# Norm and LayerNorm roots and the gated embedding kept in PSUM, with half of the residual adds of the embedding stages on GpSimd

## The chip, the cores and the metric

The kernel runs on the eight cores of one Trainium2 chip. The work is data parallel: each core has one row of 2048 prompt tokens and sixteen sequences of eight sample tokens. The metric is the device time of the slowest core in microseconds (us). Most executions agree within 0.3%. Some fall into a slower state, in which the cores of one die have a lower granted TensorE clock (the share of the full clock that the profile records), whatever the kernel is. Only fast runs are compared here, and lengths of stages are read from cores whose mean clock was 0.996 to 0.998 unless another is given. A core with such a mean can still have a lower clock within one stage; where that matters, the clock in the stage is given.

TensorE is called PE in the profile, VectorE DVE, ScalarE ACT and GpSimd POOL.

## The reference, cut to what matters

A step is two layers. Each has an FFN, a mixer, a second FFN and then a gated input embedding. The change acts mostly on that last part, which is called the embedding stage here.

```python
def rmsnorm(x, g):
    ...
    inv = lax.rsqrt(jnp.mean(xf * xf, axis=-1, keepdims=True) + NORM_EPS)
    return (xf * inv * g.astype(jnp.float32)).astype(x.dtype)
...
for i in range(DEPTH):                       # DEPTH = 2, D_MODEL = 1024
    ...                                      # FFN, mixer, FFN, each with its norm
    gate = jax.nn.sigmoid(rmsnorm(x, norm_ple[i]) @ w_ple_gate[i])
    emb = rmsnorm(p[i].astype(x.dtype) @ w_ple_proj[i], norm_ple_proj[i])
    x = x + gate * emb
y = rmsnorm(x, norm_final)
```

## The kernel before

The residual stream X stays in SBUF, transposed: eight chunks of 128 channels for each block of tokens. There are four blocks of 512 columns (x_43 to x_46 in the profile) and one sample block of 128 (x_47). The normalised input H (h_48 to h_52) feeds the matmuls. All accumulators come from a pool of eight PSUM banks, named ps.

An embedding stage does this for each chunk `mo` of each block `b`:

```python
pz, pe_ = bank(), bank()                         # two PSUM banks
mm(pz[:, 0:n], ...)                              # gate: 8 matmuls
mm(pe_[:, 0:n], ...)                             # embedding: 2 matmuls
th = scr()                                       # SBUF scratch
act(th[:, 0:n], pz[:, 0:n], AF.Tanh, scale=0.5)  # ScalarE
bfree(pz)
dve_stt(th[:, 0:n], th[:, 0:n], 1.0, pe_[:, 0:n], ALU.add, ALU.mult)      # VectorE: product
bfree(pe_)
dve_stt(X[b][:, mo, :], th[:, 0:n], GPPH[:, l * 8 + mo:l * 8 + mo + 1], X[b][:, mo, :],
        ALU.mult, ALU.add)                                                # VectorE: residual
sfree(th)
nm[b].chunk(mo, 2.8)                             # the next norm's square of this chunk
```

The last call places a square of the new X chunk into ScalarE's program, and later a matmul with a matrix of ones that sums the squares. The first argument after `mo` is a lag. It is no wait at run time. The program is written out ahead of time, with a running count of PE time, and the lag says after how much of that time the square goes into ScalarE's instruction order. A chunk is 2.38 us of PE, so a square with lag 2.8 stands a little more than a chunk behind. In the timelines below one later tanh stands between a chunk's own tanh and its square.

When all eight squares of a block are summed, the root is taken and eight products give H:

```python
self.wait = {"pe": 4.0, "dve": 1.2, "pool": 1.0}[mode]   # from the square to its sum, same clock
...
def chunk(self, mo, lag=0.8):
    ...
    defer(lag * k, square, self.tag)                     # k = 1 for 512 columns

def rsqrt(self):
    rs = scr()                                           # the root goes to SBUF
    act(rs[:, 0:n], self.pb[:, 0:n], AF.Abs_reciprocal_sqrt, bias=NORM_EPS)
    bfree(self.pb)
    st = 0.7 if n == 512 else 0.3
    ...                                                  # for c in 8: at 2.0 + st * c
    dve_stt(out[b][:, c, :], X[b][:, c, :], pcol(self.gname, c), rs[:, 0:n], ALU.mult, ALU.mult)
```

## Time and profile before

Before took 2615.22 us (median of the three fast of four runs, 2614.91 to 2615.65; the fourth was slow, 3135.62, and the median of all four is 2615.43).

From the page (the summary of the profiled execution), which is of a core of the die at clock 0.992, the engines' busy time and share of the span and, last, the chain of waits by engine:

```profile
span 2623.8 us, 34959 instructions; the slowest of 8 cores (2608.9 to 2623.8 us)
PE 2576.8 (98%) x14375; PEld 1247.0 (48%) x14375; DVE 1155.4 (44%) x2039; ACT 708.4 (27%) x1257; POOL 168.2 (6%) x254
...
PE 93%; DVE 4%; ACT 2%; DMA 1%; issue 1%; SPq 0%; ACTq 0%; POOL 0%; DVEq 0%; POOLq 0%
```

PE is nearly always busy, so only places where it waits can give time. One such place is the pair of embedding stages. Each stage is taken from the end of the second FFN's last residual add on the sample block to the end of the last gated residual add of that block. The windows view of core 1 (clock 0.997) for the two stages has each engine's busy time:

```profile
core 1: us, PE busy (x) PEld busy (x) DVE busy (x) ACT busy (x) POOL busy (x), PEclk, DMA share, GB/s
1206.90:1305.90 99.00, 95.49 (x506) 44.97 (x503) 80.55 (x139) 61.60 (x104) 5.33 (x11) 1.00 0.19 32
2510.60:2599.30 88.70, 82.78 (x441) 40.00 (x439) 74.15 (x128) 56.54 (x98) 0.46 (x1) 0.98 0.27 87
```

VectorE is busy 81% of layer 0's stage and ScalarE 62%. The waits of PE in layer 0's stage (engine, tile, what it waited for: total, times, longest) are few:

```profile
PE ps L553 <- DVE scr_96 L523: 1.5, 1, 1.5
PE ps L553 <- DVE scr_95 L523: 0.8, 1, 0.8
PE ps L553 <- DVE scr_94 L523: 0.5, 1, 0.5
```

One more of 0.5 us (`scr_93`) falls at its end.

By the timeline of PE, the eight gate matmuls of that chunk had ended at 1264.28 us, so it was held back for 6.2 us:

```profile
1262.39 1.89 PE L553 MATMUL ps<-h_51,ring 128*128 128x512 bf16 x8
...
1269.09 1.90 PE L553 MATMUL ps<-h_51,ring 128*128 128x512 bf16 x8 [1.49 <-DVE scr_96 L523]
```

The second line is the stage's longest wait of PE. It ended with a VectorE product, as the prediction has it.

### The profile page before, as it was taken

What the parts mean: (1) busy time and instruction counts of PE and PEld (TensorE: products, weight loads), DVE (VectorE), ACT (ScalarE), POOL (GpSimd) and SP (SyncE); (2) the same over time, 40 slices, a digit from 0 to 9 for tenths busy, and PEclk for the clock granted to TensorE, in tenths of its full rate; (3) what the DMA queues carried; (4) which work ended last, traced back from release to release, by engine and by line L of the source; (5) the groups of instructions that cost most, each with busy time, mean ns of one, the idle gap of its engine ahead of it and who ended that gap; (6) DMA issues with size and microseconds to landing.
All of it is one profiled execution on the core that took longest, in us unless ns stands there. A gap on an engine that the chain in (4) does not pass through costs nothing.

```text
span 2623.8 us, 34959 instructions; the slowest of 8 cores (2608.9 to 2623.8 us)
## 1 busy us (share of the span) xinstructions
PE 2576.8 (98%) x14375; PEld 1247.0 (48%) x14375; DVE 1155.4 (44%) x2039; ACT 708.4 (27%) x1257; POOL 168.2 (6%) x254
## 2 busy tenths in 40 slices
PE   7999999999999999999999999999999999999996
PEld 2444544444454454444444454445444444544443
DVE  5432334755632222268722222267667312222687
ACT  5210112336621001125521001123333210011254
POOL 0000000012400000000000000000005000000000
PEclk9999999999999999999999999999999999999998
DMA  8320421055442132112042031103310320322113
GB/s 195 55 44 1 65 37 32 16 103 122 86 69 39 18 56 38 33 29 46 7 71 41 17 60 29 33 13 49 56 33 6 57 53 17 57 37 41 21 22 137
DMA packets 53311, 127.18 MB, mean 48 GB/s; under 512 B 9504, under 2 KB 24608, under 8 KB 53024
## 3 DMA queue, kind: packets, MB, share of 16 engines
q0 software_dynamic: 23584, 92.55, 21.1%
q1 hardware_dynamic: 28848, 31.29, 4.4%
q8 instruction: 113, 1.85, 0.3%
q10 hardware_dynamic: 720, 1.11, 0.1%
q14 instruction: 46, 0.38, 0.0%
HBM read 196.61 MB, written 10.62 MB: 79 GB/s over the span
## 4 chain that ended last, share of the span: by engine, by line
PE 93%; DVE 4%; ACT 2%; DMA 1%; issue 1%; SPq 0%; ACTq 0%; POOL 0%; DVEq 0%; POOLq 0%
PE ps L553 93%; DMA x_43<-xT 0%; DVE h_48 L523 0%; DVE h_49 L523 0%; ACT L508 0%; DVE h_50 L523 0%; DVE x_46 L523 0%; DMA ring<-wts 0%; DVE x_45 L523 0%; DMA x_44<-xT 0%; DVE v L523 0%; DVE x_44 L523 0%; DVE scr_95 L516 0%; DVE h_51 L523 0%; ACT h_51 L510 0%
## 5 line engine op out<-in xcount | busy, mean ns | idle before, releaser
L553 PE MATMUL ps<-h_48,ring 128*128 128x512 bf16 x1892 | 432.5, 382 | 12.8 <-DMA ring<-wts 12.8
L553 PE MATMUL ps<-h_49,ring 128*128 128x512 bf16 x1892 | 433.2, 382 | 2.3 <-DVE h_49 L528 1.8
L553 PE MATMUL ps<-h_50,ring 128*128 128x512 bf16 x1892 | 428.8, 381 | 2.3 <-DVE h_50 L523 1.6
L553 PE MATMUL ps<-h_51,ring 128*128 128x512 bf16 x1892 | 427.7, 380 | 3.2 <-DVE scr_96 L523 1.5
L553 PEld LDWEIGHTS ps<-h_49,ring 128*128 128x128 bf16 x1892 | 185.6, 98 | 229.3 <-issue 14.6
L553 PEld LDWEIGHTS ps<-h_50,ring 128*128 128x128 bf16 x1892 | 185.4, 98 | 227.4 <-issue 8.0
L553 PEld LDWEIGHTS ps<-h_51,ring 128*128 128x128 bf16 x1892 | 184.8, 98 | 228.2 <-issue 4.7
L553 PEld LDWEIGHTS ps<-h_48,ring 128*128 128x128 bf16 x1892 | 182.2, 98 | 220.5 <-issue 23.4
L577 POOL DMA_DIRECT2D ring<-wts x152 | 80.8, 538 | 2057.4 <-PE ps L553 1967.9
L553 PE MATMUL ps<-hid_54,ring 128*128 128x512 bf16 x736 | 164.3, 380 | 0.0
L553 PE MATMUL ps<-hid_56,ring 128*128 128x512 bf16 x736 | 163.7, 379 | 0.0
L553 PE MATMUL ps<-hid_55,ring 128*128 128x512 bf16 x736 | 163.7, 379 | 0.0
L553 PE MATMUL ps<-hid_53,ring 128*128 128x512 bf16 x736 | 162.8, 379 | 0.0
L510 ACT ACTIVATE scr_97<-ps 128x512 f32<-128x512 f32 (+1 forms) x135 | 77.1, 571 | 309.5 <-PE ps L553 300.4
L510 ACT ACTIVATE scr_95<-ps 128x512 f32<-128x512 f32 (+1 forms) x130 | 67.7, 521 | 293.9 <-PE ps L553 293.9
L510 ACT ACTIVATE scr_96<-ps 128x512 f32<-128x512 f32 (+1 forms) x119 | 68.7, 577 | 241.4 <-PE ps L553 239.2
L553 PE MATMUL ps<-h_52,ring 128*128 128x128 bf16 x1892 | 124.3, 220 | 5.0 <-DVE scr_96 L523 3.1
L553 PEld LDWEIGHTS ps<-h_52,ring 128*128 128x128 bf16 x1892 | 115.0, 98 | 28.0 <-DVE scr_96 L523 3.3
L553 PEld LDWEIGHTS ps<-hid_54,ring 128*128 128x128 bf16 x736 | 72.2, 98 | 86.8 <-issue 1.2
L553 PEld LDWEIGHTS ps<-hid_56,ring 128*128 128x128 bf16 x736 | 72.0, 98 | 86.8
L553 PEld LDWEIGHTS ps<-hid_55,ring 128*128 128x128 bf16 x736 | 71.9, 98 | 86.7
L553 PEld LDWEIGHTS ps<-hid_53,ring 128*128 128x128 bf16 x736 | 71.6, 98 | 84.1
(502 smaller groups left out, 2150.3 us busy)
## 6 DMA issues: line engine op xcount, KB each, us to landing
ring<-wts POOLq DMA_DIRECT2D x110, 512.0 KB, 9.7
ring<-wts POOLq DMA_DIRECT2D x40, 768.0 KB, 8.0
rr<-u SPq DMA_DIRECT2D x48, 135.0 KB, 3.1
rr<-u SPq DMA_DIRECT2D x16, 134.8 KB, 3.5
x_44<-xT SPq DMA_DIRECT2D x8, 256.0 KB, 6.0
x_45<-xT SPq DMA_DIRECT2D x8, 256.0 KB, 11.4
x_46<-xT SPq DMA_DIRECT2D x8, 256.0 KB, 12.5
yT<-x_43 SPq DMA_DIRECT2D x8, 256.0 KB, 2.1
```

Of the source, the lines that this page charges most:

```text
L510: return e.activation(out=out, in_=in_, func=func, **kw)
L553: ins = e.matmul(o_, l, r, start=st, stop=sp)
L577: S.op(eng, lambda e: e.dma_start(out=out, in_=in_), reads=[in_], writes=[out], dma_sem=sem, dma_total=total, extra_deps=extra)
```

## The change

The intent is to take work off VectorE, which had the most to do next to PE, and to keep GpSimd's new work from disturbing it.

- Roots of the norms, of the embedding's own norm and of the LayerNorm stay in the PSUM bank that held the sum, so a norm product reads one SBUF input and one PSUM input.
- For every second 512-column chunk ScalarE scales the tanh by the gain (`gp * th + gp`), VectorE multiplies by the embedding, and GpSimd adds to the residual.
- For the other chunks the product is written back to its PSUM bank, and that bank is freed after the residual.
- The lag of the square is 4.2 for GpSimd's chunks, and the time from square to sum is 4.5.

```diff
-            self.wait = {"pe": 4.0, "dve": 1.2, "pool": 1.0}[mode]
+            self.wait = {"pe": 4.5, "dve": 1.2, "pool": 1.0}[mode]
...
-            rs = scr()
-            act(rs[:, 0:n], self.pb[:, 0:n], AF.Abs_reciprocal_sqrt, bias=NORM_EPS)
-            bfree(self.pb)
+            rs = self.pb
+            act(rs[:, 0:n], rs[:, 0:n], AF.Abs_reciprocal_sqrt, bias=NORM_EPS)
...
-                        sfree(rs)
+                        bfree(rs)
...                          (the same for the embedding's norm and the LayerNorm)
-            dve_stt(th[:, 0:n], th[:, 0:n], 1.0, pe_[:, 0:n], ALU.add, ALU.mult)
-            bfree(pe_)
-            dve_stt(X[b][:, mo, :], th[:, 0:n], GPPH[:, l * 8 + mo:l * 8 + mo + 1], X[b][:, mo, :],
-                    ALU.mult, ALU.add)
-            sfree(th)
-            nm[b].chunk(mo, 2.8)
+            gp = GPPH[:, l * 8 + mo:l * 8 + mo + 1]
+            pooled = mo % 2 == 0 and b < SB
+            if pooled:
+                act(th[:, 0:n], th[:, 0:n], AF.Identity, bias=gp, scale=gp)
+                dve_tt(th[:, 0:n], th[:, 0:n], pe_[:, 0:n], ALU.mult)
+                bfree(pe_)
+                pool_tt(X[b][:, mo, :], th[:, 0:n], X[b][:, mo, :], ALU.add)
+                sfree(th)
+            else:
+                dve_stt(pe_[:, 0:n], th[:, 0:n], 1.0, pe_[:, 0:n], ALU.add, ALU.mult)
+                sfree(th)
+                dve_stt(X[b][:, mo, :], pe_[:, 0:n], gp, X[b][:, mo, :], ALU.mult, ALU.add)
+                bfree(pe_)
+            nm[b].chunk(mo, 4.2 if pooled else 2.8)
```

More of the change, by code (lines that the diff above doesn't have):

```diff
@@ L801, in s1 @@
                 SQ.put(r)
-            rs = scr()
+            rs = pb
             act(rs[:, 0:n], pb[:, 0:n], AF.Abs_reciprocal_sqrt, bias=NORM_EPS)
-            bfree(pb)
             def s2():
@@ L808, in s2 @@
                     dve_tt(HID[b][:, k, :], pt[:, k, 0:n], rs[:, 0:n], ALU.mult)
-                sfree(rs)
+                bfree(rs)
                 if b + 2 < NB:
@@ L964, in stats @@
                     LNP.put(vv)
-                mu, msq, rs = scr(), scr(), scr()
+                mu, msq, rs = scr(), scr(), p2
                 act(mu[:, 0:n], p1[:, 0:n], AF.Copy)
@@ L972, in stats @@
                     if j == 0:
-                        dve_tt(msq[:, 0:n], p2[:, 0:n], msq[:, 0:n], ALU.subtract)
-                        bfree(p2)
-                        act(rs[:, 0:n], msq[:, 0:n], AF.Abs_reciprocal_sqrt, bias=LN_EPS)
+                        dve_tt(p2[:, 0:n], p2[:, 0:n], msq[:, 0:n], ALU.subtract)
                         sfree(msq)
+                        act(rs[:, 0:n], p2[:, 0:n], AF.Abs_reciprocal_sqrt, bias=LN_EPS)
                 sfree(mu)
@@ L983, in ln1 @@
                             scale=pcol("ln_gain", j))
-                    sfree(rs)
+                    bfree(rs)
                 defer(3.0, ln1, tag)
```

## The prediction

> **What bounds the kernel.** TensorE: the page gives PE 98% of a 2623.8 us span, and the chain of waits is 93% matmuls. The holes in the PE timeline of core 5:
> - even mixer (640 to 700 us): 3.8 us idle;
> - embedding stage of layer 0 (1208 to 1312): about 4.4 us of waits, 1.5 of it in block 3 for a VectorE product that frees a bank, most of the rest around the sample block;
> - embedding stage of layer 1 (2518 to 2610): 0.6, 1.5, then 0.6 and 3.1 us waiting for VectorE in the last, 128-column block, which spans 13.2 us for about 6 us of matmuls;
> - head (about 18 us) and tail (2610 to 2624), hardly touched.
>
> In the embedding stages a 512-column chunk costs PE 2.38 us (11 matmuls at 0.216). VectorE spends about 1.39 us on the chunk's two scalar_tensor_tensor (0.68, 0.75) plus 0.66 for one normalisation product of an earlier block, in bursts of four (2.7 us). Each norm's two table loads and root cost ScalarE about 3.2 us and starve VectorE, which recovers too slowly: PE waits in block 3, and VectorE is 3 to 5 us late at the sample block.
>
> **The change.** For half the chunks VectorE loses the 0.75 us residual and keeps one product (0.68). GpSimd gains an add of about 1.16 us (its lone adds in the even mixer). ScalarE gains a pass of about 0.80 us: the trace has 0.80 for an activation with two pointer operands, 0.72 with one, 0.60 to 0.63 with none, agreeing with the Trainium skill, "ScalarE: Activation LUTs", "What ACT_TABLE_LOAD costs" (about 93 ns per pointer). Per 512 block VectorE falls from about 16.4 to 13.5 us, ScalarE rises from about 12.5 to 15, PE stays 19.
>
> rs in PSUM does not itself speed a product (0.69 from PSUM, 0.68 from SBUF). It should remove contention: norm products that overlap GpSimd's adds average 0.87 to 0.93 (h_49, h_50) against 0.745, which fits the skill's "SBUF — State Buffer", "SBUF: two separate sides" (GpSimd locks out a VectorE op with two SBUF inputs). So the new GpSimd adds should be nearly free to VectorE.
>
> The price: each norm keeps a PSUM bank some 7 us longer. When an embedding stage starts, accumulators and roots leave about 4 banks for chunks of 2 each, while VectorE there is up to 6 us behind: 1 to 3 us of new PE waits in all, there and in the even mixer.
>
> **Sum (estimates from these numbers).** Layer 0 embedding -3 us. Layer 1: -2 at block 3, -5 at the sample block. Even mixer -1 to +1. New bank waits +2. About -8 us, 0.3%: 2607 us, range 2599 to 2616. Faster by over 2%: 1%; within 2%: 98%; slower: 1%.
>
> **What would show it.** The PE waits of block 3 vanish; the last 128-column block takes 7 to 9 us; VectorE's busy time in an embedding stage falls by about 12 us, GpSimd's rises by about 19; norm products in the even mixer return to 0.745. Signs of a wrong step: PE waiting for a norm product to free a bank; squares late behind GpSimd; residual adds well over 1.2 us.
>
> **What would make it wrong.** More bank waits than thought (then no gain or a small loss); ScalarE, in order, blocked by squares that wait for GpSimd; the later squares and sums (+0.5 us) pushing a norm onto the critical path, above all at the end, where 13 us follow the last matmul.

## More of the kernel before

A piece of core 1's (start, duration, what; in brackets the idle time before it and what ended that):

```profile
1269.92 0.63 ACT L510 ACTIVATE sq_88<-x_45 128x512 bf16<-128x512 f32 x1 [2.98 <-DVE x_45 L523]
1270.45 0.58 ACT L510 ACTIVATE scr_94<-ps 128x512 f32<-128x512 f32 x1
1271.30 0.63 ACT L510 ACTIVATE sq_92<-x_45 128x512 bf16<-128x512 f32 x1 [0.27 <-DVE x_45 L523]
1271.84 0.58 ACT L510 ACTIVATE scr_97<-ps 128x512 f32<-128x512 f32 x1
```

ScalarE stood idle for 2.98 us, because the next instruction in its order was a square (`sq_88<-x_45`) whose residual was not written yet. The tanh of a later chunk (`scr_94<-ps`) followed at once after it.

## The result, and the profile after

After took 2620.6 us (median of four fast runs, 2620.39 to 2622.42), against 2615.22. The ratio is 1.0022, with a 95% interval of 1.0002 to 1.0042. Here and below a ratio is the mean time of one kernel's fast runs over that of the other's fast runs of the same rounds, so it is not quite the ratio of the medians quoted. The total lies within 2%, as the prediction said was likely, but on the wrong side: 5 us slower where 8 us faster was expected, and above the range.

The page after, the slowest core, now at clock 0.997:

```profile
span 2619.2 us, 34719 instructions; the slowest of 8 cores (2613.9 to 2619.2 us)
PE 2551.5 (97%) x14124; PEld 1243.5 (47%) x14375; DVE 1122.7 (43%) x2007; ACT 731.5 (28%) x1289; POOL 205.2 (8%) x286
...
PE 88%; DVE 5%; ACT 3%; DMA 2%; issue 1%; POOL 0%; ACTq 0%; DVEq 0%; SPq 0%; POOLq 0%
```

This trace lacks 251 matmul records (14124 of 14375), so PE's smaller busy time means nothing. The work moved as planned: VectorE has 32.7 us less, ScalarE 23.1 us more, GpSimd 37.0 us more. In the chain PE's share fell by 5 points, a part of which may come from the missing records; VectorE, ScalarE and DMA gained one point each, as rounded.

The windows view of core 1 for the two embedding stages after:

```profile
1203.10:1305.80 102.70, 95.56 (x504) 44.74 (x503) 70.03 (x123) 73.18 (x120) 25.20 (x26) 1.00 0.19 31
2510.00:2601.20 91.20, 82.78 (x440) 39.91 (x438) 63.71 (x113) 68.07 (x114) 20.83 (x17) 0.98 0.27 84
```

VectorE lost 10.5 us in layer 0's stage and 10.4 us in layer 1's, and yet the stages grew from 99.0 to 102.7 us and from 88.7 to 91.2 us. The other stages give at most a little back: the even mixer took 204.1 to 205.5 us on the four cores of die 0 before and 203.5 to 205.0 us after, and the tail went from 14.2 to 14.0 us (core 1). The FFNs and the odd mixer are equal within the spread of their cores.

The waits of PE in layer 0's stage after, where the sum is 7.1 us against 3.3 us before:

```profile
PE ps L553 <- DVE x_47 L523: 2.1, 4, 0.6
PE ps L553 <- DVE h_49 L523: 1.5, 1, 1.5
PE ps L553 <- DVE h_51 L523: 1.2, 1, 1.2
PE ps L553 <- ACT scr_93 L510: 0.8, 1, 0.8
PE ps L553 <- DVE scr_95 L516: 0.8, 1, 0.8
PE ps L553 <- ACT scr_97 L510: 0.4, 1, 0.4
PE ps L553 <- DVE h_50 L523: 0.3, 1, 0.3
```

Three kinds are new. PE waits for norm products (`h`), which free the root's bank, for residuals (`x_47`), which free the product's bank, and for tanh (`ACT scr`), which free the gate's bank.

The timelines of core 1 show how a tanh comes late. PE, ScalarE, VectorE and GpSimd, one fence each:

```profile
1261.84 1.89 PE L553 MATMUL ps<-h_51,ring 128*128 128x512 bf16 x8
...
1265.84 1.90 PE L553 MATMUL ps<-h_51,ring 128*128 128x512 bf16 x8 [1.47 <-DVE h_49 L523]
```

```profile
1263.73 0.58 ACT L510 ACTIVATE scr_96<-ps 128x512 f32<-128x512 f32 x1
1267.83 0.63 ACT L510 ACTIVATE sq_88<-x_45 128x512 bf16<-128x512 f32 x1 [3.52 <-POOL x_45 L519]
1268.37 0.58 ACT L510 ACTIVATE scr_93<-ps 128x512 f32<-128x512 f32 x1
```

```profile
1263.07 2.71 DVE L523 SCALAR_TENSOR_TENSOR h_49<-x_44,par,ps 128x512 bf16<-128x512 f32 x4
1265.70 0.68 DVE L516 TENSOR_TENSOR scr_97<-scr_97,ps 128x512 f32<-128x512 f32 x1
...
1269.83 0.69 DVE L516 TENSOR_TENSOR scr_93<-scr_93,ps 128x512 f32<-128x512 f32 x1 [2.05 <-ACT scr_93 L510]
```

```profile
1266.53 1.27 POOL L519 TENSOR_TENSOR x_45<-scr_97,x_45 128x512 f32<-128x512 f32 x1 [5.33 <-DVE scr_97 L516]
```

Read them as one chain. The gate matmuls of the first PE line ended at 1263.73 us, and their tanh is `scr_93`. The product of `scr_97` stood behind a burst of four norm products on VectorE. GpSimd could then start its add, and ended at 1267.80. Only then could ScalarE do the square of that chunk, for which it had stood idle 3.52 us. The tanh of `scr_93` came after the square, 4.6 us after its matmuls, and VectorE, whose next instruction was the product of `scr_93`, stood idle 2.05 us for the scaled `scr_93`. PE in the meantime had run out of banks: its next gate waited 1.47 us for the same burst of norm products, whose root held the bank. VectorE's idle time in the stage rose from 99.0 - 80.6 = 18.4 us to 102.7 - 70.0 = 32.7 us, so it was not short of time.

### The profile page after: what moved, and what is told of

Its sections match the earlier page's. It is cut to its first block, busy times and chain, and to the rows that moved or that the text cites. A ratio compares the mean times of both kernels' runs of the same rounds, so it can differ in the third digit from the quotient of the medians.

```text
span 2619.2 us, 34719 instructions; the slowest of 8 cores (2613.9 to 2619.2 us)
## 1 busy us (share of the span) xinstructions
PE 2551.5 (97%) x14124; PEld 1243.5 (47%) x14375; DVE 1122.7 (43%) x2007; ACT 731.5 (28%) x1289; POOL 205.2 (8%) x286
## 4 chain that ended last, share of the span: by engine, by line
PE 88%; DVE 5%; ACT 3%; DMA 2%; issue 1%; POOL 0%; ACTq 0%; DVEq 0%; SPq 0%; POOLq 0%
PE ps L553 88%; ACT L508 1%; DMA ring<-wts 1%; DVE h_50 L523 1%; DVE h_51 L523 1%; DVE x_46 L523 0%; DMA x_43<-xT 0%; DVE ps L523 0%; DMA xscr_67<-st_sc 0%; DVE v L523 0%; ACT scr_93 L510 0%; DVE h_49 L523 0%; ACT ps L510 0%; DVE h_48 L523 0%; DVE x_45 L523 0%
## 5 line engine op out<-in xcount | busy, mean ns | idle before, releaser
L553 PE MATMUL ps<-h_48,ring 128*128 128x512 bf16 x1835 | 419.1, 380 | 19.9 <-DMA ring<-wts 14.9
L553 PE MATMUL ps<-h_49,ring 128*128 128x512 bf16 x1844 | 424.3, 379 | 6.5 <-DVE h_51 L523 2.6
L553 PE MATMUL ps<-h_50,ring 128*128 128x512 bf16 x1873 | 424.8, 379 | 5.7 <-ACT scr_93 L510 1.6
L553 PE MATMUL ps<-h_51,ring 128*128 128x512 bf16 x1841 | 423.2, 379 | 6.8 <-DVE x_44 L523 1.5
L553 PEld LDWEIGHTS ps<-h_51,ring 128*128 128x128 bf16 x1892 | 184.5, 98 | 227.9 <-DVE x_44 L523 2.0
L553 PEld LDWEIGHTS ps<-h_50,ring 128*128 128x128 bf16 x1892 | 184.6, 98 | 227.4 <-ACT scr_93 L510 2.5
L553 PEld LDWEIGHTS ps<-h_49,ring 128*128 128x128 bf16 x1892 | 184.4, 98 | 226.8 <-DVE h_51 L523 3.5
L553 PEld LDWEIGHTS ps<-h_48,ring 128*128 128x128 bf16 x1892 | 181.3, 98 | 223.4 <-issue 16.4
L553 PE MATMUL ps<-hid_56,ring 128*128 128x512 bf16 x720 | 162.9, 379 | 0.9
L553 PE MATMUL ps<-hid_54,ring 128*128 128x512 bf16 x720 | 162.9, 379 | 0.8
L553 PE MATMUL ps<-hid_55,ring 128*128 128x512 bf16 x723 | 162.7, 379 | 0.6
L553 PE MATMUL ps<-hid_53,ring 128*128 128x512 bf16 x720 | 161.4, 379 | 0.8
L510 ACT ACTIVATE scr_93<-ps 128x512 f32<-128x512 f32 (+1 forms) x118 | 61.9, 524 | 355.9 <-PE ps L553 352.1
L510 ACT ACTIVATE scr_96<-ps 128x512 f32<-128x512 f32 (+1 forms) x118 | 67.0, 568 | 228.4 <-PE ps L553 226.6
L553 PEld LDWEIGHTS ps<-h_52,ring 128*128 128x128 bf16 x1892 | 114.8, 98 | 27.1 <-DVE x_45 L523 2.5
L510 ACT ACTIVATE scr_95<-ps 128x512 f32<-128x512 f32 (+1 forms) x101 | 51.7, 511 | 239.3 <-PE ps L553 229.1
L510 ACT ACTIVATE scr_94<-ps 128x512 f32<-128x512 f32 (+1 forms) x102 | 58.0, 568 | 206.3 <-PE ps L553 196.9
L553 PEld LDWEIGHTS ps<-hid_55,ring 128*128 128x128 bf16 x736 | 72.0, 98 | 86.8
L553 PEld LDWEIGHTS ps<-hid_56,ring 128*128 128x128 bf16 x736 | 72.0, 98 | 86.9
L553 PEld LDWEIGHTS ps<-hid_54,ring 128*128 128x128 bf16 x736 | 72.1, 98 | 86.5
```

What stands on the lines that cost most here:

```text
L510: return e.activation(out=out, in_=in_, func=func, **kw)
L553: ins = e.matmul(o_, l, r, start=st, stop=sp)
```

## The experiments

Two explanations stood against each other from the start.

- **Queue**: ScalarE runs its instructions in order, and a square that waits for a late residual holds back later tanh, and with them their banks. The change makes the residual later, so it should hold more of them. The Trainium skill, "PSUM — Partial Sum Buffer", section "Engine vs sequencer instructions", says that the queues of ScalarE, VectorE and GpSimd are strict FIFO. The timelines above agree, with their 2.98 and 3.52 us.
- **Banks**: roots and products that stay in PSUM take banks from PE's rotation.

A third one, that ScalarE simply has too much work (its pass), was kept as a rival too. The table has what the runs showed in layer 0's stage, on one undisturbed core each, and is the map for what follows. "Blocked" is ScalarE's idle time that ended with a residual (the sum of those lines of its waits in the stage), "starved" its idle time that ended with PE, and "PE waits" sums PE's waits. "Held" is the mean time from the end of a chunk's eight gate matmuls to the start of its tanh, over the 32 chunks of 512 columns, worked out from the timelines of PE and ScalarE.

| kernel | layer 0 stage | layer 1 stage | ScalarE busy | blocked | starved | PE waits | held |
|---|---|---|---|---|---|---|---|
| before (lag 2.8) | 99.0 | 88.7 | 61.6 | 33.6 | 2.2 | 3.3 | 2.6 |
| after | 102.7 | 91.2 | 73.2 | 25.5 | 2.1 | 7.1 | 2.5 |
| e1: after, norm root in SBUF | 104.9 | 94.6 | 73.0 | 29.7 | 0 | 8.4 | 3.9 |
| e2: before + norm root in PSUM | 100.9 | 89.7 | 61.6 | 33.1 | 4.6 | 5.4 | 1.8 |
| e3: before + GpSimd adds alone | 105.4 | 94.5 | 73.0 | 29.3 | 1.3 | 8.0 | 4.3 |
| e6: after, add on VectorE | 103.5 | 95.4 | 73.6 | 24.8 | 3.1 | 7.7 | 2.1 |
| e16: before + product in PSUM | 99.8 | 90.7 | 61.7 | 33.7 | 2.8 | 4.6 | 2.3 |
| e17: before + ScalarE's pass alone | 101.0 | 91.4 | 73.3 | 25.6 | 0.3 | 3.7 | 3.2 |
| e14: before, lag 1.4 | 120.5 | 111.0 | 61.7 | 57.2 | 0.9 | 20.2 | 6.5 |
| e10: before, lag 5.2 | 95.4 | 85.5 | 61.5 | 8.1 | 24.8 | 0.8 | 0.6 |
| e15: e10 + spread norm products | 94.0 | 84.8 | 61.1 | 2.9 | 27.5 | 0.8 | 0.6 |
| e5: after, lags 8.0 and 5.2 | 96.5 | 85.8 | 73.5 | 4.9 | 16.7 | 2.8 | 0.8 |

The clock in the layer 0 stage was 1.000 in every row but e14's (0.986; e14 takes 120.4 us on cores at 1.000). In layer 1 it differed: 0.946 in e6, 0.962 to 0.969 in e1, e3, e14, e16 and e17, 0.98 in before, after, e2 and e10, 1.000 in e5 and e15. So that column holds for before against after, and is not to be read to less than about 1 us elsewhere.

Add busy and blocked in the rows with early squares: 61.6 + 33.6 = 95.2 of 99.0 us before, 73.2 + 25.5 = 98.7 of 102.7 us after, 118.9 of 120.5 us with lag 1.4. ScalarE, 62% busy before, had hardly any time left in which it could have taken a ready tanh. With late squares the tanh is held for 0.6 to 0.8 us, and PE's waits nearly go. The last two columns also have a trap: after holds its tanh no longer than before (2.5 and 2.6 us), yet PE waits twice as long. The same hold meets fewer free banks, because roots and products now stay in them, and PE stops earlier. So the two explanations are not exclusive, and the runs were to say how much each weighs.

### First batch: the parts of the change

**e1: the whole change, norm root back in SBUF.**

```diff
-            rs = self.pb
-            act(rs[:, 0:n], rs[:, 0:n], AF.Abs_reciprocal_sqrt, bias=NORM_EPS)
+            rs = scr()
+            act(rs[:, 0:n], self.pb[:, 0:n], AF.Abs_reciprocal_sqrt, bias=NORM_EPS)
+            bfree(self.pb)
...
```

> The changed kernel with one part undone: the root of the eight-chunk norm (class Norm) goes back to an SBUF scratch tile and its bank is freed at once; everything else of the change stays. Measure: length of the embedding stage of layer 0, from the end of the sample block's last down-projection add to the end of its last gated residual, on a die at clock 0.997: 99.0 us in the kernel before, 102.7 in the changed one; for layer 1: 88.7 and 91.5. Theory 1 (PSUM banks: roots and gated products kept in PSUM shorten the rotation, PE waits for a free bank): 96 to 99 us and total 2 to 8 us under the changed kernel. Rival 2 (ScalarE, in order: extra scale pass and squares that wait for GpSimd delay the tanh that frees a bank): stays at 102 to 103. Rival 3 (later squares and sums, wait 4.5 and lag 4.2): stays at 102 to 103.

Measured: 1.0039 of before (1.0024 to 1.0054; fast runs 2630.8 to 2631.6 us, before 2619.3 to 2622.9 on that chip). Layer 0's stage took 104.9 us, 2.2 us more than after, and more than any of the three theories expected. So banks held by the norm root are not what made the change slow as a whole: giving them back made it slower. With GpSimd adding, the root in PSUM is a help (e17 below has the likely reason).

**e2: before, with the norm root in PSUM and nothing else.**

```diff
-            rs = scr()
-            act(rs[:, 0:n], self.pb[:, 0:n], AF.Abs_reciprocal_sqrt, bias=NORM_EPS)
-            bfree(self.pb)
+            rs = self.pb
+            act(rs[:, 0:n], rs[:, 0:n], AF.Abs_reciprocal_sqrt, bias=NORM_EPS)
...
```

> The kernel before with one part of the change alone: the root of the eight-chunk norm stays in its PSUM bank until the last product. Theory 1 (banks): embedding stage of layer 0 rises from 99.0 to 101 to 104 us, total 3 to 8 us over before. Rivals 2 and 3 (ScalarE order, later sums): unchanged at 98.5 to 99.5 us, total within 1 us of before.

Measured: 1.0011 (0.9998 to 1.0024), which alone decides nothing, but layer 0's stage took 100.9 us on the undisturbed cores 4, 5 and 7 against 99.0. The waits of PE have the reason, in this line of core 5:

```profile
PE ps L553 <- DVE h L523: 2.9, 2, 2.2
```

PE waited 2.9 us for norm products to free a bank. Banks do cost, about 2 us here, which is just under what the bank theory expected (101) and more than its rivals allowed (99.5).

**e3: before, with ScalarE's pass and GpSimd's adds, roots and products in SBUF.**

```diff
+            if pooled:
+                act(th[:, 0:n], th[:, 0:n], AF.Identity, bias=gp, scale=gp)
+                dve_tt(th[:, 0:n], th[:, 0:n], pe_[:, 0:n], ALU.mult)
+                bfree(pe_)
+                pool_tt(X[b][:, mo, :], th[:, 0:n], X[b][:, mo, :], ALU.add)
...
-            nm[b].chunk(mo, 2.8)
+            nm[b].chunk(mo, 4.2 if pooled else 2.8)
```

> The kernel before with only the pooled half of the change: every second residual add on GpSimd, ScalarE scaling the gate, lag 4.2 for those chunks; all roots and the unpooled product stay in SBUF as before, wait 4.0. Theory 1 (banks): the relief of VectorE shows; embedding stage of layer 0 falls to 94 to 97.5 us, layer 1 to 82 to 87, total 4 to 10 us under before. Rival 2 (ScalarE order): 101 to 103 us, total 2 to 6 us over before. Side check: norm products (root in SBUF) that overlap a GpSimd add should take 0.87 us or more against 0.745 alone.

Measured: 1.0042 (1.0029 to 1.0056), layer 0's stage 105.4 us. The pass and the adds alone cost more than the whole change, and more than either theory expected.

**e4: the whole change without GpSimd's part.**

```diff
-            pooled = mo % 2 == 0 and b < SB
+            pooled = False
```

> The changed kernel with pooling switched off (all chunks take the unpooled branch, lag 2.8), roots and gated product in PSUM, wait 4.5. Theory 1 (banks): embedding stage of layer 0 at 102 to 107 us, as slow as the changed kernel or slower because VectorE has its full load again. Rival 2 (ScalarE order): back to 98 to 99.5 us. Rival 3 (later sums): between, above 99.

Measured: 1.0026 (1.0013 to 1.0038), layer 0's stage 102.45 us on the three cores whose clock in the stage was 1.000, and 104.1 to 104.3 us on the five where it was 0.974 to 0.984. So 102.45 us is the value to compare. This is what the bank theory expected, and the queue theory had expected 98 to 99.5. The PSUM part without GpSimd is slow too. So each half of the change costs, and the two don't add: +6.4 us in e3, +3.5 us here, +3.7 us together.

### Second batch: what makes the squares late

**e5: the whole change, squares later.**

```diff
-            nm[b].chunk(mo, 4.2 if pooled else 2.8)
+            nm[b].chunk(mo, 8.0 if pooled else 5.2)
```

> The first four runs refuted banks as the sole cause: pooling alone costs more (105.4 us in the embedding stage of layer 0) than roots in PSUM alone (101.0). New theory A: ScalarE works in program order; a square of a pooled chunk is issued 4.2 us after its matmuls and sits at the head of ScalarE's queue until VectorE's product and GpSimd's add are done, and behind it the tanh of later chunks, which frees banks, waits. This run is the changed kernel with the squares issued later in program order: lag 8.0 for pooled and 5.2 for unpooled chunks instead of 4.2 and 2.8. Theory A: the embedding stage of layer 0 falls from 102.7 to 95 to 99.5 us, layer 1 from 91.4 to 84 to 89, total at or under the kernel before. Rival B (the extra ScalarE pass as load: 16 x 0.81 us per stage): stays at 102 to 103. Rival C (later squares and sums themselves hurt): rises above 104.

Measured: layer 0's stage 96.5 us and layer 1's 85.8 to 86.9 us (die 0, clock 0.997 and 0.998; the other die of that run was slow). Five of the six timed runs were slow; the one fast run took 2610.98 us (undisturbed runs of before on that chip 2615.6 and 2616.3). With the same work on every engine, the change became 6.2 us shorter in layer 0's stage by a shift of ScalarE's order. Too much work on ScalarE falls as a cause by itself with this: ScalarE is as busy as in after (73.5 against 73.2 us).

**e6: the whole change, with the add on VectorE.**

```diff
-                pool_tt(X[b][:, mo, :], th[:, 0:n], X[b][:, mo, :], ALU.add)
+                dve_tt(X[b][:, mo, :], th[:, 0:n], X[b][:, mo, :], ALU.add)
```

> The changed kernel with the pooled residual add on VectorE instead of GpSimd; ScalarE's scale pass, lags and PSUM roots stay. Theory A (squares wait for GpSimd at the head of ScalarE's queue): 99 to 101 us in the embedding stage of layer 0, ScalarE's wait for squares shorter, VectorE's load higher. Rival B (ScalarE's pass as load): 102 to 105, no better than the changed kernel.

Measured: layer 0's stage 103.5 us on the two cores at 1.000 in the stage, 104.8 us on six at 0.984, so 0.8 us longer than with GpSimd (102.7 at 1.000). The queue theory had expected 99 to 101 and was wrong here. The ratio (0.9979, 0.9839 to 1.012) says nothing, because before was noisy in that batch. Inside the whole change GpSimd's add is not what costs: its 1.27 us latency is no worse than VectorE's extra load.

**e8: before, with only the changed delays.**

```diff
-            self.wait = {"pe": 4.0, "dve": 1.2, "pool": 1.0}[mode]
+            self.wait = {"pe": 4.5, "dve": 1.2, "pool": 1.0}[mode]
...
-            nm[b].chunk(mo, 2.8)
+            nm[b].chunk(mo, 4.2 if mo % 2 == 0 and b < SB else 2.8)
```

> The kernel before with the change's delays alone: wait 4.5 instead of 4.0, lag 4.2 for every second chunk of the 512-column blocks; no arithmetic moved, no bank held longer. Theory A and rival B: 97 to 99.5 us in the embedding stage of layer 0 (later squares do no harm, by theory A they help a little). Rival C (delays hurt): 101 us or more.

Measured: layer 0's stage 99.3 us, as before (99.0), and fast runs at 2616.5 us. Later squares on half of the chunks did no harm and did not help.

**e10: before, with all squares late.**

```diff
-            nm[b].chunk(mo, 2.8)
+            nm[b].chunk(mo, 5.2)
```

> The kernel before with lag 5.2 instead of 2.8 for the squares of all chunks in the embedding stages. Theory A: ScalarE no longer waits for VectorE's residuals in front of a tanh (30 us of such waits in the kernel before, in a window of 90), so the embedding stage of layer 0 falls from 99.0 to 94.5 to 97.5 us, and total 2 to 8 us under before. Rival B: 98.5 to 99.5. Rival C: above 100.

Measured: layer 0's stage 95.4 us on all cores, layer 1's 84.8 to 86.8 us. The two fast runs took 2607.3 and 2607.4 us; the ratio (0.9911, 0.9772 to 1.005) is wide, since before's four fast runs there spread from 2615.6 to 2651.4 us, two of them at 2615.6 and 2616.3. One number in the kernel before gained about what the change was meant to gain. ScalarE's waits in layer 0's stage (core 1) changed their kind, from late residuals to an empty queue:

```profile
ACT scr L510 <- PE ps L553: 23.1, 25, 2.2
ACT sq L510 <- DVE x L523: 8.1, 7, 3.2
```

### Third batch: the size of the effect, and its mix with the banks

**e14: before, with squares earlier.**

```diff
-            nm[b].chunk(mo, 2.8)
+            nm[b].chunk(mo, 1.4)
```

> The kernel before with lag 1.4 instead of 2.8: squares earlier in ScalarE's program order, nothing else. Theory A (a square at the head of ScalarE's queue that waits for its residual holds up the next tanh): the wait of ScalarE for residuals grows above 27 us in the window 1215 to 1290, and the embedding stage of layer 0 rises from 99.0 to 101 to 108 us, layer 1 from 88.7 to 90 to 97. If order does not matter: 99 and 89.

Measured: 1.0169 (1.0153 to 1.0185), layer 0's stage 120.5 us. First ScalarE's waits, then PE's, in that stage of core 1:

```profile
ACT sq L510 <- DVE x L523: 57.2, 35, 2.9
```

```profile
PE ps L553 <- ACT sq L510: 16.9, 25, 1.6
```

That is above the 101 to 108 us that the queue theory expected. The trace also shows a second way from the squares to PE: in its timeline these 16.9 us are waits before the matmuls that sum the squares (`ps<-sq,ones`), and not before a bank. PE stood there with the next matmuls behind in its order.

With this the lag's effect is a series: 1.4, 2.8 and 5.2 gave 120.5, 99.0 and 95.4 us, with the same arithmetic on every engine. ScalarE was busy 61.7, 61.6 and 61.5 us, and blocked 57.2, 33.6 and 8.1 us. That the place of the squares sets the length of these stages is shown, not only argued. The lag moves the sums, the roots and the norm products behind the squares as well; their part was not separated.

**e13: e10, with the norm products spread.**

```diff
-            st = 0.7 if n == 512 else 0.3
+            st = (1.5 if self.mode == "pe" else 0.7) if n == 512 else 0.3
...
-            nm[b].chunk(mo, 2.8)
+            nm[b].chunk(mo, 5.2)
```

> A candidate to beat both: the kernel before with squares of the embedding stages at lag 5.2, and the eight norm products of those stages spread (one per 1.5 us of TensorE time instead of 0.7), so that VectorE no longer runs four of them (2.7 us) in front of a chunk's own two operations. With lag 5.2 alone the stages took 95.4 and 85.4 us and the only large PE wait left was 3.3 us for VectorE in the last sample block, behind such a burst. Expected: layer 0 at 94.5 to 95.5 us, layer 1 at 82 to 85.5, total 7 to 13 us under before. If bursts do not matter: as with lag 5.2 alone, 95.4 and 85.4, total 7 to 9 us under before.

Measured: layer 0's stage 94.0 us and layer 1's 84.8 us (with a clock of 1.000 there, at which e10's core 7 took 84.8 us too), but 0.9991 (0.9975 to 1.0007) in all. The first FFN took 521 to 526 us against 514 to 518, since its norms use the same mode and their products were spread as well. That was a mistake of the edit; e15 below mends it.

**e11: e5, with the norm root in SBUF**, and **e12: e10, with the norm root in PSUM.**

```diff
 e11, against the change:
-            rs = self.pb
-            act(rs[:, 0:n], rs[:, 0:n], AF.Abs_reciprocal_sqrt, bias=NORM_EPS)
+            rs = scr()
+            act(rs[:, 0:n], self.pb[:, 0:n], AF.Abs_reciprocal_sqrt, bias=NORM_EPS)
+            bfree(self.pb)
...
-            nm[b].chunk(mo, 4.2 if pooled else 2.8)
+            nm[b].chunk(mo, 8.0 if pooled else 5.2)
 e12, against before: the edit of e2, and
-            nm[b].chunk(mo, 2.8)
+            nm[b].chunk(mo, 5.2)
```

> The changed kernel with late squares (8.0 and 5.2) and the norm root back in SBUF. With late squares and the root in PSUM the stages took 96.5 and 86.5 us, and PE waited 1.3 us for a norm product at the start of each (a bank held by a root). Banks: that wait goes; layer 0 falls to 95 to 96 us. GpSimd contention (a norm product with two SBUF inputs blocked by a GpSimd add): products rise from 0.74 to 0.9 us or more; if that matters for TensorE the stage stays at or above 96.5 us.

> The kernel before with late squares (5.2) and the norm root kept in PSUM; no pooling. Banks as a cost of their own: layer 0 rises from 95.4 (late squares, root in SBUF) to 96.5 to 98 us, layer 1 from 85.4 to 86 to 88, with a PE wait for a norm product. If banks only cost where ScalarE is held up: 95.4 and 85.4.

Measured: e11 0.9985 (0.997 to 0.9999), stages 95.9 and 87.7 to 89.0 us; e12 stages 95.6 and 85.6 to 87.1 us, three fast runs at 2607.8 to 2609.5 us and a fourth, called fast, at 2645.7 us, which makes its ratio (1.0014, 0.9948 to 1.008) useless. With late squares the root in PSUM costs 0.2 us in layer 0 (95.6 against e10's 95.4), where it cost 2 us with early ones (e2). e11 lost PE's wait for a norm product, as the bank theory expected, and its norm products took 872 ns. So a bank's price depends on whether the squares are early; that the held tanh are the reason (1.8 us in e2, 0.5 us in e12) is argued.

### Fourth batch: the terms one by one, and a better kernel

**e16: before, with only the product kept in PSUM.**

```diff
-            dve_stt(th[:, 0:n], th[:, 0:n], 1.0, pe_[:, 0:n], ALU.add, ALU.mult)
-            bfree(pe_)
...                          (and the old residual; lag 2.8 stays)
+                dve_stt(pe_[:, 0:n], th[:, 0:n], 1.0, pe_[:, 0:n], ALU.add, ALU.mult)
+                sfree(th)
+                dve_stt(X[b][:, mo, :], pe_[:, 0:n], gp, X[b][:, mo, :], ALU.mult, ALU.add)
+                bfree(pe_)
```

> The kernel before with one edit: the gated product is written to its PSUM bank, which comes free after the residual op and not before it; no pooling, norm root in SBUF. If longer use of banks by the product costs: layer 0's embedding takes 100 to 102 us against 99.0. If it costs nothing: 98.5 to 99.5 us.

Measured: 99.8 us on every core (one look, not timed; two cores were disturbed in the first FFN, but not in this stage). The cost is 0.8 us, below the 1 to 3 us that the bank theory asked for and above the 0.5 us of no cost. PE's waits in the stage, core 1, are now all for residuals:

```profile
PE ps L553 <- DVE x L523: 4.6, 8, 1.5
```

**e17: before, with ScalarE's pass, and product and add on VectorE.**

```diff
+                act(th[:, 0:n], th[:, 0:n], AF.Identity, bias=gp, scale=gp)
+                dve_tt(th[:, 0:n], th[:, 0:n], pe_[:, 0:n], ALU.mult)
+                bfree(pe_)
+                dve_tt(X[b][:, mo, :], th[:, 0:n], X[b][:, mo, :], ALU.add)
...                          (every second chunk; the others as before)
+            nm[b].chunk(mo, 4.2 if pooled else 2.8)
```

> The kernel before with ScalarE's scale pass on every second chunk, but product and residual add both on VectorE; root and product in SBUF. If ScalarE's pass in the path from matmul to residual is what pooling costs: layer 0's embedding takes 103 to 106 us, as with pooling alone (105.4). If GpSimd's add (its time, or its use of SBUF beside VectorE) is what costs: 99 to 100.5 us.

Measured: 101.0 us on all cores (one look). Neither expectation held: the pass costs 2.0 us (with the lag of 4.2, whose own effect was 0.3 us in e8), and GpSimd's add in place of VectorE's another 4.4 us (105.4 in e3). PE's waits grew by only 0.4 us. The rest is in stops too short for the waits view: where the starts of two matmuls lie further apart than the usual 216 ns (512 columns) or 56 ns (128), the excess sums to 4.9 us before and 6.9 us in e17, and 1.1 and 2.3 us of it are stops that the view leaves out. For the other 4.4 us, groups of instructions by line in 1215 to 1290 us point to a cause (count | busy, mean ns). First e3, core 5, then e17, core 1, then the whole change, core 1 (one tile of each kind):

```profile
L523 DVE SCALAR_TENSOR_TENSOR h<-x,par,scr 128x512 bf16<-128x512 f32 x24 | 19.8, 872 | 0.0
L519 POOL TENSOR_TENSOR x<-scr,x 128x512 f32<-128x512 f32 x14 | 19.4, 1388 | 56.6 <-DVE scr L516 56.6
L523 DVE SCALAR_TENSOR_TENSOR x<-scr,gpph,x 128x512 f32<-128x512 f32 x14 | 12.7, 909 | 0.5
```

```profile
L523 DVE SCALAR_TENSOR_TENSOR h<-x,par,scr 128x512 bf16<-128x512 f32 x24 | 16.6, 745 | 0.0
L523 DVE SCALAR_TENSOR_TENSOR x<-scr,gpph,x 128x512 f32<-128x512 f32 x15 | 11.3, 752 | 0.5
```

```profile
L523 DVE SCALAR_TENSOR_TENSOR h_48<-x_43,par,ps 128x512 bf16<-128x512 f32 x8 | 5.5, 743 | 0.0
L523 DVE SCALAR_TENSOR_TENSOR x_44<-ps,gpph,x_44 128x512 f32<-128x512 f32 x4 | 3.0, 751 | 0.1
L519 POOL TENSOR_TENSOR x_43<-scr_97,x_43 128x512 f32<-128x512 f32 x2 | 2.5, 1270 | 9.4 <-DVE scr_97 L516 9.4
```

The same VectorE ops, both with two inputs in SBUF, took 872 and 909 ns beside GpSimd's adds, and 745 and 752 ns without them. In the whole change, where each has an input in PSUM, they took 742 and 751 ns on average, and GpSimd's add 1270 ns instead of 1388. And there, the same swap of VectorE's add for GpSimd's gained 0.8 us (e6 against after), where it cost 4.4 us here. This is what the Trainium skill says in "SBUF — State Buffer", section "SBUF: two separate sides": GpSimd and a VectorE op with two SBUF inputs share an exclusively locked pair of ports. The traces agree.

**e15: before, late squares and spread products, the first FFN's norms left alone.**

```diff
-            st = 0.7 if n == 512 else 0.3
+            st = (1.5 if self.mode == "pe" and self.gname != "norm_ffn00" else 0.7) if n == 512 else 0.3
...
-            nm[b].chunk(mo, 2.8)
+            nm[b].chunk(mo, 5.2)
```

> The kernel before with squares 5.2 us after their chunk and the norm products of the embedding stages 1.5 us apart, the norm of the first FFN left as it was. Theory (ScalarE's queue is blocked by early squares, and bursts of norm products delay the residuals): layer 0's embedding takes about 94.0 us, layer 1's about 84.8 us, the first FFN is back at 514 to 518 us, and the whole is 8 to 11 us under the kernel before. Rival (the stage gains are paid back in the FFN that follows, whose first matmuls wait for late norm products): the stages are as short, but the total is within 3 us of the kernel before.

Measured: 0.996 of before (0.9943 to 0.9978; three fast runs at 2606.1 to 2608.1 us, before ten at 2615.5 to 2619.4 us). The stages took 94.0 and 84.8 us, the first FFN 514 to 518 us. It is correct, and it beats before by 9.7 us in the means (2606.8 against 2616.5), and so also the changed kernel, though the two were not run side by side. The gain is that of the lag: e10's two fast runs took 2607.3 and 2607.4 us. The spreading took 1.4 us from layer 0's stage (95.4 to 94.0), but the FFN behind it took 475.7 us against e10's 474.4. For the spreading, the rival's account is right.

## Why the prediction was wrong

The layer 0 stage can be built up from before to after by steps of these runs: 99.0 before; 101.0 with ScalarE's pass and the lag of 4.2 (e17); 105.4 with the adds on GpSimd (e3); 104.9 with the product, the embedding's root and the LayerNorm's root in PSUM, and the wait of 4.5 (e1); 102.7 with the norm root in PSUM (after). In that order the change costs +2.0, +4.4, -0.5 and -2.2 us, together +3.7 where -3 was predicted.

- **The step that failed: "ScalarE rises from about 12.5 to 15, PE stays 19", and with it that VectorE's load is what limits the embedding stages.** The busy numbers were right: ScalarE rose by 11.6 us in layer 0's stage, 2.9 us per block, and VectorE fell by 10.5 us. What was wrong is to read the rest of 15 of 19 us as room. ScalarE was already busy or blocked for 95.2 of 99.0 us before. The change put 0.81 us of scaling and a 1.27 us add behind a product into the path from a matmul to its residual, and the square at a lag of 4.2 in front of later tanh. The prediction names this under what would make it wrong, "ScalarE, in order, blocked by squares that wait for GpSimd", but gave it no term in its sum. The lag series and e5 show what it is worth: the same change with late squares takes 96.5 us, 6.2 us less. Against before with late squares (e10, 95.4 us; the lags are not quite the same) the change then costs 1.1 us and not 3.7, so by this difference about 2.6 of its 3.7 us exist only while the squares are early.
- **"Layer 0 embedding -3 us. Layer 1: -2 at block 3, -5 at the sample block."** Measured: +3.7 and +2.5 us. The wait in block 3 did not vanish. It was 1.5 us for a product (`scr_96`) and became 1.5 us for a norm product (`h_49`): the bank that PE wanted had another owner, served by the same burst on VectorE. At layer 1's sample block PE waited 0.6 and 3.1 us for VectorE before, and 0.8 and 2.3 us after, so 0.6 us were gained there of the 5 predicted. VectorE with less work was not earlier, because it waited for ScalarE more: its waits in layer 0's stage that ended with ScalarE rose from 13.8 to 25.9 us.
- **"New bank waits +2."** Right in kind: the trace of after shows just the sign named, PE waiting for `h`, 1.5, 1.2 and 0.3 us. Their size is not one number: the root alone costs 1.9 us in layer 0's stage (e2) and the product alone 0.8 us (e16), with early squares, and the root costs 0.2 us with late ones (e12). That shorter rotation and held tanh act together is my reading of the last two columns of the table; the runs show the parts, not each bank.
- **"So the new GpSimd adds should be nearly free to VectorE."** Right: norm products 742 ns, unpooled residuals 751 ns. Without the roots and products in PSUM they were 872 and 909 ns (e3). The add took 1.27 us where 1.16 was predicted.
- **Even mixer -1 to +1, tail.** Right: on core 3, which is at 0.997 in both, 204.1 to 203.5 us (die 0: 204.1 to 205.5 before, 203.5 to 205.0 after), and the norm products of blocks 0 to 2 fell to 742 ns, as predicted (from 782, 782 and 1119 ns, core 1). The tail did not suffer (14.2 to 14.0 us).
- **The sum.** -8 us predicted. Measured on the medians of the fast runs: +5.4 us, of which the two stages are 3.7 + 2.5 = 6.2 us, less about 0.8 us in even mixer and tail.

What stays open is how the fewer free banks and the held tanh share the loss in the whole change. And the change is not rescued by late squares: e5 is still 1.1 us longer in layer 0's stage than e10 (96.5 against 95.4), and 1.3 us of PE's 2.8 us of waits there are for a norm product that frees a bank; with that root in SBUF (e11) it is 95.9 us, but then layer 1 loses more. Taking VectorE's load off bought nothing, even there. What the change would do with spread products besides was not run.

## What to carry to other kernels

Before you call an engine's idle share room, look at what ends its idle time: an engine that executes in order and stands before an operand that is not ready has none, whatever its busy share. When a change lengthens the path to a value, move every later consumer of that value down its queue with it, and try the order alone, in the kernel before, as a first experiment. Here that was one number, and worth more than the change.

## What the Trainium skill lacked or had wrong

- "Perfetto Trace Analysis", section "Identifying the Most-Contended Engine", says to find the bottleneck by occupancy, for Vector and Scalar engines too. Among those two that points at VectorE in the embedding stage here (80.6 of 99.0 us, ScalarE 61.6), and the change that took 10.5 us off VectorE made the stage 3.7 us longer. ScalarE's blocked time (33.6 us) had to be added to its busy time. The section "Optimization Strategy" of that page, which says to look for what blocks an engine's gaps, would have led there, if applied to ScalarE.
- "PSUM — Partial Sum Buffer", section "Engine vs sequencer instructions", states the strict FIFO, but no page says what it can cost: with lags of 1.4, 2.8 and 5.2 the same instructions took 120.5, 99.0 and 95.4 us.
- "VectorE: DVE Perf Modes", section on the TRN2 errata, gives a VectorE op from PSUM 120 fixed cycles and one from SBUF 58, and says itself that the 58 is too low for a single op. It has no row for an op with one input in each. Here it made no such difference to move one of two SBUF inputs to PSUM: norm products 742 against 746 ns, residuals 751 against 752 ns.
- "SBUF — State Buffer", section "SBUF: two separate sides", has the rule for the locked ports and was right. That section has no size for a mix of ops: here 17% on norm products and 21% on residuals beside GpSimd's adds (872 over 745 ns, 909 over 752 ns), and 9% on the add itself (1388 over 1270 ns).
